# Two down projections by seven block products in place of eight

## The chip, the cores and the metric

The kernel runs on one core of one Trainium2 chip. The metric is the device time of the whole program in microseconds (us): the median of the runs.

## The reference

A trunk of two decoder layers on 512 tokens with 1024 features, in float32. Each layer mixes tokens in three branches (RWKV-7, retention, spatial gating), merges them by gates, and then runs a gated MLP with a causal convolution. The change is in the last product of that MLP:

```python
def conv_ffn(h, w_up, conv_w, conv_b, w_down):
    S = h.shape[1]
    u = h @ w_up
    up = jnp.pad(u, ((0, 0), (CONV_WIDTH - 1, 0), (0, 0)))
    c = conv_b
    for j in range(CONV_WIDTH):
        c = c + conv_w[j] * up[:, j:j + S]
    gate, val = jnp.split(c, 2, axis=-1)
    return (jax.nn.silu(gate) * val) @ w_down

# per layer, after the mixer:
x = x + conv_ffn(rmsnorm(x, norm2_g[l]), ffn_w_up[l], ffn_conv_w[l], ffn_conv_b[l], ffn_w_down[l])
# after both layers:
return rmsnorm(x, final_g)
```

`w_down` has 2816 rows (22 blocks of 128) and 1024 columns, so a down projection is (512 x 2816) by (2816 x 1024).

## The kernel before

The stream between layers is kept by features: eight tiles `x[m]` of 128 features by 512 tokens. A float32 product is made of three matmuls in the rounded type fp32r (`mm3`): each operand is split into a high part (a copy on ACT that rounds) and a low part (a subtraction on DVE), and the products high by low, high by high and low by high are added in PSUM. `unit` fetches a weight block of 128x512 by a DMA on SP's queue (`load`), splits it (`part`), and runs ahead of its use by a plan that a first pass over the program has noted; how far ahead depends on the pool (`AHEAD`). The order in which each engine gets its instructions is set by the Tile scheduler, except where `keep_in_program_order` fixes it.

Buffers of 128x512 float32: `u` has 31, `r` 16, `f` 39 (the MLP's), the split weights `wh` and `wl` three each. PSUM has four banks named `acc` and four named `sm`.

`ffn_up` makes 22 tiles of activations (128 features by 512 tokens). For each of the two columns of a tile it evacuates PSUM (L1054, DVE), applies the convolution (L1056 on ACT, L1057 and L1058 on DVE), then the gate (L1062 to L1064), and splits the result into `ah` tiles (L1066 ACT, L1067 DVE).

`ffn_down` (layer 0) has the weights as stationary operand and the activations as moving operand: for each of the eight output tiles, 22 blocks by three matmuls of 512 token columns, 528 in all. Behind each tile DVE adds it to x (L1078), and the norm of the next layer is prepared (`norm_z`, `norm_sq`).

`last` (layer 1) turns it around, so that the output has tokens in the partitions: a block of 128 tokens of the activations is stationary, and 512 output features of the weights are moving; 2 halves by 22 blocks by 4 token blocks by 3, 528 matmuls. The last `KEPT` blocks of the second half are done token block by token block, so that the final norm and the output of one overlap with the products of the next.

## Time and profile before

| | |
|---|---|
| Median of three runs | 1715.23 us (1712.87 to 1715.34) |
| Profiled execution, first to last instruction | 1712.1 us |
| Granted TensorE clock, mean | 1.000 |
| Layer 0 down projection on TensorE | 738.8 to 858.6 us |
| Layer 1 down projection on TensorE | 1585.8 to 1705.6 us |
| Behind the last matmul | 6.5 us |

For the profiled execution the page gives its span and no other time. PE is TensorE's matmuls, PEld its weight loads, DVE VectorE, ACT ScalarE, POOL GpSimd, SP the engine that issues most DMAs. A row for a group of instructions gives the line of the kernel, the engine, the operation, output and inputs by the program's names, the shape and the count, then busy time and the mean duration of one in ns; where a row answers a question on one line, it has the shortest, median and longest duration. A row of the timeline begins with the start in us and the duration in us; "x4" at its end says that four instructions are merged.

### The profile page before, as it was taken

Reading aid. Unit: us, or ns where it says so; the run is one execution under the profiler, and the core shown is the slowest. Engines: PE = TensorE matmul, PEld = TensorE weight load, DVE = VectorE, ACT = ScalarE, POOL = GpSimd, SP = SyncE. Lnnn points to the kernel's source line nnn. Section 1 sums busy time; section 2 is a strip of 40 time slices with the busy share of each in tenths; the row PEclk is TensorE's granted clock in tenths of the full one; section 3 lists DMA queues with packets and bytes.
Section 4 is the critical chain, followed back from the end, with each engine's and each line's share of the span. In section 5 each row is a group of like instructions: output and inputs, shape, how many; then the busy total and the mean of one; then the engine's idle time right before and its main releaser. Section 6 shows DMA issues by size and latency. Waiting matters only on the chain.

```text
span 1712.1 us, 27377 instructions
## 1 busy us (share of the span) xinstructions
PE 1701.0 (99%) x10280; PEld 1392.4 (81%) x10280; DVE 1155.0 (67%) x1998; ACT 774.9 (45%) x1315; POOL 178.2 (10%) x213
## 2 busy tenths in 40 slices
PE   9999999999999999999999999999999999999998
PEld 7888777788888888888888888777888888888886
DVE  6887745578669777753368887555776787787333
ACT  6563443554255444433355634345533554444223
POOL 2121000003200000000021210100141011100010
PEclk9999999999999999999999999999999999999999
DMA  5236553525542333233432365535254433333333
GB/s 180 87 109 205 174 174 99 178 89 163 163 148 93 98 99 96 69 113 114 123 105 87 107 222 168 159 122 178 77 185 147 137 122 117 113 109 99 99 99 105
DMA packets 132325, 219.61 MB, mean 128 GB/s; under 512 B 16864, under 2 KB 37088, under 8 KB 132192
## 3 DMA queue, kind: packets, MB, share of 16 engines
q1 hardware_dynamic: 116336, 180.94, 34.4%
q0 software_dynamic: 6784, 20.98, 3.8%
q10 hardware_dynamic: 9072, 15.94, 2.6%
q8 instruction: 81, 1.33, 0.3%
q14 instruction: 52, 0.43, 0.1%
HBM read 188.43 MB, written 29.36 MB: 127 GB/s over the span
## 4 chain that ended last, share of the span: by engine, by line
PE 89%; DMA 5%; DVE 3%; ACT 1%; issue 1%; SPq 1%; ACTq 0%; POOL 0%; DVEq 0%; POOLq 0%
PE acc L152 80%; PE sm L152 4%; PE sm L640 2%; DMA wr<-wall 2%; PE sm L893 1%; DVE wl L136 1%; PE sm L547 1%; DMA ws<-sgw 1%; DMA tr<-yt 0%; DMA tr<-bkT 0%; SPq L226 0%; DMA bkS<-tr 0%; PE sm L998 0%; DMA x<-xT 0%; DMA tr<-qkt 0%
## 5 line engine op out<-in xcount | busy, mean ns | idle before, releaser
L152 PE MATMUL acc<-hi,sh 128*128 128x512 f32 x1108 | 431.9, 390 | 0.0
L152 PE MATMUL acc<-lo,sh 128*128 128x512 f32 x1108 | 431.6, 390 | 0.0
L152 PE MATMUL acc<-hi,sl 128*128 128x512 f32 x1108 | 430.6, 390 | 0.0
L135 ACT CAST sh<-wr 128x512 fp32r<-128x512 f32 (+1 forms) x347 | 212.2, 615 | 356.6 <-PE acc L152 264.3
L136 DVE TENSOR_TENSOR sl<-wr,sh 128x512 fp32r<-128x512 f32 (+1 forms) x347 | 236.1, 683 | 139.9 <-ACT sh L135 74.9
L136 DVE TENSOR_TENSOR wl<-wr,wh 128x512 fp32r<-128x512 f32 x233 | 165.2, 710 | 184.9 <-ACT wh L135 182.3
L135 ACT CAST wh<-wr 128x512 fp32r<-128x512 f32 x233 | 144.1, 619 | 281.1 <-PE acc L152 182.3
L152 PEld LDWEIGHTS acc<-hi,sl 128*128 128x128 f32 x1108 | 208.0, 188 | 43.7 <-DVE gth L1013 0.3
L152 PEld LDWEIGHTS acc<-lo,sh 128*128 128x128 f32 x1108 | 208.0, 188 | 43.6 <-issue 0.9
L152 PEld LDWEIGHTS acc<-hi,sh 128*128 128x128 f32 x1108 | 208.0, 188 | 43.6 <-issue 0.3
L152 PE MATMUL acc<-lo,wh 128*128 128x512 f32 x588 | 232.5, 395 | 0.5 <-DVE lo L211 0.3
L152 PE MATMUL acc<-hi,wl 128*128 128x512 f32 x588 | 230.3, 392 | 0.5 <-DVE wl L136 0.5
L152 PE MATMUL acc<-hi,wh 128*128 128x512 f32 x588 | 229.5, 390 | 0.0
L152 PEld LDWEIGHTS acc<-lo,wh 128*128 128x128 f32 x588 | 110.5, 188 | 26.3 <-DVE lo L211 1.6
L152 PEld LDWEIGHTS acc<-hi,wl 128*128 128x128 f32 x588 | 110.5, 188 | 25.9 <-DVE wl L136 2.3
L152 PEld LDWEIGHTS acc<-hi,wh 128*128 128x128 f32 x588 | 110.6, 188 | 22.4 <-issue 0.2
L152 PE MATMUL acc<-ah,sh 128*128 128x512 f32 x352 | 108.4, 389 | 0.0
L1054 DVE TENSOR_TENSOR fu<-acc,rsF 128x512 f32<-128x512 f32 x88 | 60.6, 688 | 56.4 <-PE acc L152 56.3
L1056 ACT ACTIVATE cv<-fu,pc 128x512 f32<-128x512 f32 x88 | 71.6, 816 | 46.7 <-DVE fu L1054 44.4
L1057 DVE SCALAR_TENSOR_TENSOR cv<-fu,pc,cv 128x511 f32<-128x511 f32 x88 | 65.8, 748 | 21.1 <-ACT cv L1056 20.6
L152 PE MATMUL acc<-wl,hi 128*128 128x512 f32 x192 | 78.3, 408 | 0.0
L152 PEld LDWEIGHTS acc<-ah,sh 128*128 128x128 f32 x352 | 66.1, 188 | 13.7
(312 smaller groups left out, 2345.4 us busy)
## 6 DMA issues: line engine op xcount, KB each, us to landing
wr<-wall SPq DMA_DIRECT2D x488, 256.0 KB, 2.7
gd<-gth ACTq DMA_DIRECT2D x48, 256.0 KB, 3.0
gth<-gd POOLq DMA_DIRECT2D x48, 256.0 KB, 3.6
wr<-wdt SPq DMA_DIRECT2D x44, 256.0 KB, 2.6
wr<-wdn SPq DMA_DIRECT2D x40, 256.0 KB, 2.7
tr<-bkT SPq DMA_DIRECT2D x16, 256.0 KB, 2.8
bkS<-tr SPq DMA_DIRECT2D x128, 32.0 KB, 2.5
tr<-vT SPq DMA_DIRECT2D x8, 256.0 KB, 2.6
```

What stands on the lines that cost most here:

```text
L135: self.kept(self.nc.scalar.copy(hi[:, :n], raw[:, :n]))
L136: self.kept(self.nc.vector.tensor_tensor(lo[:, :n], raw[:, :n], hi[:, :n], op=SUB))
L152: i = self.nc.tensor.matmul(*x, **y)
L547: i = T.matmul(pK[hv[1 - h], j, :], bk[hv[h], c, 1, :], x[hv[h], c, :], start=True, stop=True)
L640: po(T.matmul(o, l, r, start=start, stop=True, skip_group_check=True))
L893: po(T.matmul(X[h][:, i, :], lhsT, rhs, start=new[h], stop=stop, skip_group_check=True))
L1054: V.tensor_tensor(u, ps, self.rsF, op=MUL)
L1056: A.activation(t, u, AF.Identity, scale=self.p("cw2", j), bias=self.p("cb", j))
L1057: V.scalar_tensor_tensor(t[:, 1:], u[:, :511], self.p("cw1", j), t[:, 1:], op0=MUL, op1=ADD)
```

## The change

Both down projections are computed by the seven-product scheme of Strassen and Winograd on 2x2 blocks: the 512 tokens are halved (256 each), the 22 row blocks of the weights are taken as eleven pairs `q` (even and odd block), and the output features are halved. Each weight block of a pair is called b11, b12, b21, b22; four of the seven products (numbers 7, 5, 6, 4 in the code) take sums of weight blocks and sums of activation halves, three (1, 2, 3) take plain blocks or one sum.

- In `ffn_up`, `halves` makes the sums of activation halves for each pair on POOL, splits two of the resulting tiles into `act`, and writes the plain first halves (`ab`) and one more sum (`s4`) to DRAM by DMAs on POOL's queue. They are read back later and split (`back`, `back4`, and their like in `last`).
- `sums` loads four raw weight blocks, forms three sums on POOL and one on DVE, in place, and `ring` splits each.
- Layer 0: four blocks `m` of output features (a pair of x tiles each), each in three groups of 4, 4 and 3 pairs `q`. A first phase of 12 steps makes products 7, 5, 6, 4 and adds them into x; a second phase makes products 1, 3, 2 from plain weights, loaded again. The weights are stationary, and a matmul has 256 token columns. The output tiles come in the order 1, 0, 3, 2, and so on.
- Layer 1: the activations are stationary as before, with 512 features in a product. A first phase over the eleven `q` makes products 7, 5, 6, 4 for two token blocks each in all eight PSUM banks; then product 1, then 3 and 2. Token blocks 2 and 3 are finished after product 1; blocks 0 and 1 at the end, with `KEPT` of 5 in place of 6.
- A `stage` number keeps `unit` from loading the next layer's weights before the end of layer 0's down projection.

The weights of layer 0 are laid out for this in DRAM. The diff without the end of `last`, which keeps the old links for the norm and the output, and some helpers:

```diff
-KEPT = 6
+KEPT = 5
...
+            if u[6] > self.stage or self.npart > at and (self.npart - at > AHEAD[u[5]] or u[5] == "f" and self.fp is None):
                 break
-            while self.nraw < min(self.npart + NRAW, len(self.plan)):
+            while self.nraw < min(self.npart + NRAW, len(self.plan)) and self.plan[self.nraw][6] <= self.stage:
...
-            hi, lo = at(), at()
-            A.copy(hi, th)
-            V.tensor_tensor(lo, th, hi, op=SUB)
-            act.append((hi, lo))
+            if i % 2 == 0:
+                even = th
+            else:
+                act.append(self.halves(even, th, i // 2, at))
         return act
 
+    def halves(self, a, b, q, at):
+
+        P, h = self.nc.gpsimd, [slice(0, 256), slice(256, 512)]
+        s, d = [self.wp.tile([128, 512], F32, name=self.nm(t), tag=t, bufs=3) for t in ("wh", "wl")]
+        P.tensor_tensor(s[:, h[0]], a[:, h[1]], b[:, h[1]], op=ADD)
+        P.tensor_tensor(s[:, h[1]], s[:, h[0]], a[:, h[0]], op=SUB)
+        P.tensor_tensor(d[:, h[0]], b[:, h[0]], s[:, h[1]], op=SUB)
+        ab = self.dp.tile([128, 512], F32, name=self.nm("ab"))
+        if q % 2 == 0:
+            self.s4 = self.dp.tile([128, 512], F32, name=self.nm("s4"))
+        for o, i in ((ab[:, h[0]], a[:, h[0]]), (ab[:, h[1]], b[:, h[0]]), (self.s4[:, h[q % 2]], d[:, h[0]])):
+            P.dma_start(o, i)
+        P.tensor_tensor(b[:, h[0]], a[:, h[0]], a[:, h[1]], op=SUB)
+        return self.split(s, at), self.split(b, at), ab, self.s4
 
     def ffn_down(self, l, act, x, st):
-        nc, V = self.nc, self.nc.vector
+        nc, V, A, P, po = self.nc, self.nc.vector, self.nc.scalar, self.nc.gpsimd, self.tc.keep_in_program_order
         self.load_pc(l + 1)
-        xd = []
-        for m in range(8):
-            ps = self.acc()
-            self.matF(ps, ("wdn", l, m, 0), act)
-            V.scalar_tensor_tensor(x[m], ps, 0.5, x[m], op0=MUL, op1=ADD)
-            self.norm_z(st, x[m], "n1")
+        Q, G, h = NFF // 2, [range(0, 4), range(4, 8), range(8, 11)], [slice(0, 256), slice(256, 512)]
+        self.pin = True
+        nring = [0]
+
+        def ring(w, n):
+            nring[0] += 1
+            if nring[0] % 2:
+                hi, lo = [self.wp.tile([128, 512], F32R, name=self.nm(t), tag=t, bufs=3) for t in ("wh", "wl")]
+            else:
+                hi, lo = [self.u(dt=F32R, n=t) for t in ("sh", "sl")]
+            A.copy(hi[:, :n], w[:, :n])
+            V.tensor_tensor(lo[:, :n], w[:, :n], hi[:, :n], op=SUB)
+            return hi, lo
+
+        def raw(m, j, i, g, al):
+            w, n = al(n="raw"), 128 * len(G[g])
+            po(nc.sync.dma_start(w[:, :n], self.a["wdn"][l, m, j, i][:, 512 * g:512 * g + n]))
+            return w
+
+        def sums(m, g):
+
+            n = 128 * len(G[g])
+            b12, b22, b11, b21 = [raw(m, j, i, g, self.r) for j, i in ((0, 1), (1, 1), (0, 0), (1, 0))]
+            c = lambda t: t[:, :n]
+            P.tensor_tensor(c(b22), c(b22), c(b12), op=SUB)
+            P.tensor_tensor(c(b12), c(b12), c(b11), op=SUB)
+            V.tensor_tensor(c(b11), c(b11), c(b22), op=ADD)
+            P.tensor_tensor(c(b21), c(b21), c(b11), op=SUB)
+            return [ring(w, n) for w in (b22, b12, b11, b21)]
+
+        def prod(ps, w, xs, new):
+            for i, (q, (x, at)) in enumerate(xs):
+                ws, cs = slice(128 * i, 128 * i + 128), slice(at, at + 256)
+                self.mm3(ps, (w[0][:, ws], w[1][:, ws]), (x[0][:, cs], x[1][:, cs]), new and i == 0, q == Q - 1, skip_group_check=True)
+
+        ab, s4 = {}, {}
+
+        def back(q, al):
+            o = self.u(n="ab")
+            nc.sync.dma_start(o, act[q][2])
+            ab[q] = self.split(o, al)
+
+        def back4(q, n):
+            o, hi, lo = self.u(n="s4"), self.f(dt=F32R, n="hi"), self.f(dt=F32R, n="lo")
+            nc.sync.dma_start(o[:, :n], act[q][3][:, :n])
+            A.copy(hi[:, :n], o[:, :n])
+            P.tensor_tensor(lo[:, :n], o[:, :n], hi[:, :n], op=SUB)
+            s4[q] = s4[q + 1] = hi, lo
+
+        steps = [(m, g) for m in range(4) for g in range(3)]
+        W = [sums(*steps[0])]
+        for n, (m, g) in enumerate(steps):
+            if n + 1 < len(steps):
+                W.append(sums(*steps[n + 1]))
+            if g == 0:
+                pa, pb = self.acc(), self.acc()
+                out = {7: pa[:, h[0]], 6: pa[:, h[1]], 5: pb[:, h[0]], 4: pb[:, h[1]]}
+            w = dict(zip((7, 5, 6, 4), W.pop(0)))
+            for p in (7, 5, 6, 4):
+                i, at = {7: (1, 0), 5: (0, 0), 6: (0, 256), 4: (1, 256)}[p]
+                prod(out[p], w[p], [(q, (act[q][i], at)) for q in G[g]], g == 0 and p in (7, 5))
+            if m == 2:
+                back(g, self.r)
+            elif m == 3:
+                for q in ((3, 4, 5), (6, 7), (8, 9, 10))[g]:
+                    back(q, self.r if q == 3 else self.f)
+            if g < 2:
+                continue
+            v, x0, x1 = self.f(n="v") if m == 3 else self.u(n="v"), x[2 * m], x[2 * m + 1]
+            two = lambda t: t.rearrange("p (a t) -> p a t", a=2)
+            twice = lambda t: t.unsqueeze(1).to_broadcast([128, 2, 256])
+            A.activation(v[:, h[0]], out[6], AF.Copy, scale=0.5)
+            V.scalar_tensor_tensor(v[:, h[1]], out[7], 0.5, v[:, h[0]], op0=MUL, op1=ADD)
+            V.scalar_tensor_tensor(two(x1), twice(out[5]), 0.5, two(x1), op0=MUL, op1=ADD)
+            V.scalar_tensor_tensor(x0[:, h[1]], out[4], 0.5, x0[:, h[1]], op0=MUL, op1=ADD)
+            P.tensor_tensor(x1, x1, v, op=ADD)
+            P.tensor_tensor(x0[:, h[1]], x0[:, h[1]], v[:, h[1]], op=ADD)
+        for q in range(0, Q, 2):
+            back4(q, min(512, 256 * (Q - q)))
+        order = [(m, p, g) for m in range(4) for p in (1, 3, 2) for g in range(3)]
+        todo, units = iter(order), []
+
+        def more(n):
+            for _, (m, p, g) in zip(range(n), todo):
+                j, i = {1: (0, 0), 2: (1, 0), 3: (1, 1)}[p]
+                units.append(ring(raw(m, j, i, g, self.f), 128 * len(G[g])))
+
+        def finish(m):
+            self.norm_z(st, x[m], "n1", m)
             self.norm_sq(st, x[m])
             d = self.dp.tile([128, 512], F32, name=self.nm("xd"))
             nc.gpsimd.dma_start(d, x[m])
-            xd.append(d)
+            xd[m] = d
+
+        xd, st["z"] = [None] * 8, [None] * 8
+        more(2)
+        for m, p, g in order:
+            more(1)
+            x0, x1 = x[2 * m], x[2 * m + 1]
+            if p != 2 and g == 0:
+                ps = self.sm((128, 256))
+                one = ps if p == 1 else one
+            o = one if p == 2 else ps
+            prod(o, units.pop(0), [(q, {1: (ab[q], 0), 2: (ab[q], 256), 3: (s4[q], q % 2 * 256)}[p]) for q in G[g]], g == 0 and p != 2)
+            if g < 2:
+                continue
+            if p == 1:
+                V.scalar_tensor_tensor(two(x1), twice(o), 0.5, two(x1), op0=MUL, op1=ADD)
+                V.scalar_tensor_tensor(x0[:, h[1]], o, 0.5, x0[:, h[1]], op0=MUL, op1=ADD)
+            elif p == 3:
+                V.scalar_tensor_tensor(x1[:, h[0]], o, 0.5, x1[:, h[0]], op0=MUL, op1=ADD)
+                finish(2 * m + 1)
+                if m == 3:
+                    self.stage += 1
+                    if self.plan:
+                        pool, self.pool = self.pool, None
+                        self.ahead(len(self.used))
+                        self.pool = pool
+            else:
+                V.scalar_tensor_tensor(x0[:, h[0]], o, 0.5, x0[:, h[0]], op0=MUL, op1=ADD)
+                finish(2 * m)
+        self.pin = False
...
+        def sums(q):
+
+            b12, b22, b11, b21 = [raw(2 * q + j, n) for j, n in ((0, 1), (1, 1), (0, 0), (1, 0))]
+            P.tensor_tensor(b22, b22, b12, op=SUB)
+            P.tensor_tensor(b12, b12, b11, op=SUB)
+            V.tensor_tensor(b11, b11, b22, op=ADD)
+            P.tensor_tensor(b21, b21, b11, op=SUB)
+            return [ring(w) for w in (b22, b12, b11, b21)]
...
+        pss = {p: [(self.acc if p in (7, 5) else self.sm)() for _ in range(2)] for p in (7, 5, 6, 4)}
+        W, ab = [sums(0)], []
...
+        for q in range(Q):
+            if q + 1 < Q:
+                W.append(sums(q + 1))
+            s, t = act[q][:2]
+            w = dict(zip((7, 5, 6, 4), W.pop(0)))
+            for p in (7, 5, 6, 4) if q < Q - 1 else (6, 7, 5, 4):
+                x, at = {7: (t, 0), 5: (s, 0), 6: (s, 256), 4: (t, 256)}[p]
+                for r in range(2):
+                    prod(pss[p][r], x, at, r, w[p], q == 0, q == Q - 1)
+            o = self.u(n="ab")
+            nc.sync.dma_start(o, act[q][2])
+            ab.append(self.split(o, self.f))
...
+        seq = [(1, q) for q in range(Q)]
+        k0 = Q - KEPT
+        for g in range(0, k0, 3):
+            seq += [(p, q) for p in (3, 2) for q in range(g, min(g + 3, k0))]
+        kept = [(p, q) for p in (2, 3) for q in range(k0, Q)]
...
+        ahead(3)
+        v1, v2, v3 = [], [], []
+        for r in range(2):
+            e, f, g = [self.f(n=t) for t in ("v1", "v2", "v3")]
+            A.activation(e, pss[6][r], AF.Copy, scale=0.5)
+            plus(f, pss[7][r], e)
+            plus(g, pss[5][r], e)
+            plus(e, pss[4][r], f)
+            plus(f, pss[5][r], f)
+            addx(e, 0, 2 + r)
+            addx(f, 1, 2 + r)
+            addx(g, 1, r)
+            v1.append(e), v2.append(f), v3.append(g)
+        one = [self.sm() for _ in range(2)]
+        out = {1: one, 2: one, 3: [self.acc() for _ in range(2)]}
+        for p, q in seq:
+            ahead(1)
+            for r in range(2):
+                go(p, q, r, units[p, q])
+            if (p, q) != (1, Q - 1):
+                continue
+            for r in range(2):
+                plus(v3[r], one[r], v3[r])
+                plus(v1[r], one[r], v1[r])
+                plus(v2[r], one[r], v2[r])
...
```

More of the change, by code (lines that the diff above doesn't have):

```diff
@@ new lines, in last, with ring, raw @@
+        ss = self.small((128, NC), "fss", 1)
+        self.pin = True
+        nring = [0]
+        def ring(w):
+            nring[0] += 1
+            if nring[0] % 2:
+                hi, lo = [self.wp.tile([128, 512], F32R, name=self.nm(t), tag=t, bufs=3) for t in ("wh", "wl")]
+            else:
+                hi, lo = [self.u(dt=F32R, n=t) for t in ("sh", "sl")]
+            A.copy(hi, w)
+            V.tensor_tensor(lo, w, hi, op=SUB)
+            return hi, lo
+        def raw(k, h):
+            w = self.u(n="raw")
+            po(nc.sync.dma_start(w, self.a["wdt"][0, k][:, H[h]]))
+            return w
@@ new lines, in last, with ahead @@
+        kept = [(p, q) for p in (2, 3) for q in range(k0, Q)]
+        units, todo = {}, iter(seq + kept)
+        def ahead(n):
+            for _, (p, q) in zip(range(n), todo):
+                w = raw(2 * q + (p > 1), p == 3)
+                if (p, q) in kept:
+                    hi, lo = [self.u(dt=F32R, n=t) for t in ("sh", "sl")]
+                    A.copy(hi, w)
+                    V.tensor_tensor(lo, w, hi, op=SUB)
+                    units[p, q] = hi, lo
+                else:
+                    units[p, q] = ring(w)
@@ new lines, in go, with addx, plus @@
+        def go(p, q, r, w):
+            x, at = {1: (ab[q], 0), 2: (ab[q], 256), 3: (s4[q // 2], q % 2 * 256)}[p]
+            prod(out[p][r], x, at, r, w, q == 0 and p != 2, q == Q - 1, skip_group_check=p < 3)
+        def addx(y, h, c):
+            for j in range(4):
+                b = y[:, 128 * j:128 * j + 128].rearrange("p (a d) -> p a d", d=32)
+                P.tensor_tensor(b, b, self.xt[4 * h + j][:, c], op=ADD)
+        def plus(y, ps, z, rows=slice(0, 512)):
+            return V.scalar_tensor_tensor(y[:, rows], ps[:, rows], 0.5, z[:, rows], op0=MUL, op1=ADD)
```

151 lines of the change are left out of this document (78 added, 73 removed).

## The prediction

> **What bounds the kernel now.** I read the page first (engine totals, then the chain that ended last), then the table of busy time by stretch for the stages that the change touches, then single instructions.
>
> ```profile
> PE 1701.0 (99%) x10280; PEld 1392.4 (81%) x10280; DVE 1155.0 (67%) x1998; ACT 774.9 (45%) x1315; POOL 178.2 (10%) x213
> PE 89%; DMA 5%; DVE 3%; ACT 1%; issue 1%; SPq 1%; ACTq 0%; POOL 0%; DVEq 0%; POOLq 0%
> ```
>
> TensorE is busy for 99% of the span and carries 89% of the chain. Fewer or shorter matmuls shorten the kernel as long as nothing else becomes late. The next rows are the two down projections, first by the instructions that read the activations (`ah`), then with all engines; the third stretch of the second fence is the first 119.8 us before the second layer's down projection, still up projection.
>
> ```profile
> 738.80:858.70 119.90, 119.80 (x528) 98.87 (x527) 0.69 (x1) 0.62 (x1) 1.00 0.40 118
> 1585.80:1705.60 119.80, 119.80 (x528) 98.91 (x527) 0.69 (x1) 0.62 (x1) 1.00 0.30 97
> ```
>
> ```profile
> 738.80:858.70 119.90, 119.90 (x531) 99.28 (x530) 48.20 (x81) 38.20 (x65) 3.78 (x7) 1.00 0.40 118
> 1585.80:1705.60 119.80, 119.80 (x529) 98.91 (x527) 43.14 (x82) 36.49 (x65) 5.95 (x4) 1.00 0.30 97
> 1466.00:1585.80 119.80, 119.80 (x530) 99.01 (x528) 93.99 (x145) 55.19 (x87) 7.64 (x14) 1.00 0.36 109
> 1705.60:1712.10 6.50, 0.04 (x1) 0.00 (x0) 2.09 (x8) 2.22 (x7) 0.00 (x0) 0.90 0.42 151
> ```
>
> Columns: stretch, length, PE, PEld, DVE, ACT, POOL, granted clock, DMA share, GB/s. Each down projection is 528 matmuls of 512 columns in 119.8 us, so 0.227 us each, at the full granted clock and without a gap. DVE is busy there for 40%, POOL for 3 to 5%. There is room beside TensorE, and the question is whether the change needs more than that room.
>
> **Removed: one product in eight.** Layer 1 goes from 528 to 7 x 11 x 2 x 3 = 462 matmuls of 512 columns: 462 x 0.227 = 104.9 us, 15.0 us less. Layer 0 goes to 7 x 11 x 4 x 3 = 924 matmuls of 256 columns. No 256-column product of this type is in the trace. The nearest rows:
>
> ```profile
> 372.82 1.87 PEld L998 LDWEIGHTS sm<-ws,sgv 128*128 128x128 f32 x15
> 373.05 1.72 PE L998 MATMUL sm<-ws,sgv 128*128 128x128 f32 x14
> L998 PEld LDWEIGHTS sm<-ws,sgv x64: 187/192/192, 372.8 to 1241.7; 128*128 128x128 f32 x64
> L998 PE MATMUL sm<-ws,sgv x64: 270/275/275, 373.0 to 1241.8; 128*128 128x128 f32 x64
> ```
>
> Here weight blocks of 128x128 follow each other every (1.72 - 0.27) / 13 = 0.111 us although one load lasts 0.19, so loads overlap and a new block each 0.111 us is possible. Half of the 512-column time is 0.1135 us. Ends: 0.111 below, 0.188 above (no overlap of loads at all); I take 0.1135, because the row with overlapping loads is the nearest. Layer 0: 924 x 0.1135 = 104.9, again 15.0 us less. "TensorE: Matmul & The Clock Gate" of the Trainium skill (section Back-to-back issue gap) gives N / 2.4 + 2.5 ns, 216 ns for 512 and 109 for 256 columns. The trace has 227 for 512, so the page is 5% low here; by it layer 0 would take 100.9 and the sum would be 4 us lower. Both layers together: -30.0 us, if TensorE stays fed.
>
> **Added: sums and splits.** For each group of blocks the code now builds three weight sums on POOL and one on DVE, then splits four results (ACT copy, DVE subtract). Before, a block had only a copy and a subtract. The costs:
>
> ```profile
> L1016 POOL TENSOR_TENSOR gth<-gth,gth x16: 1277/1292/1670, 408.6 to 1302.2; 128x512 f32<-128x512 f32 x16
> L136 DVE TENSOR_TENSOR sl<-wr,sh x347: 417/685/1155, 46.7 to 1689.1; 128x512 fp32r<-128x512 f32 x166, 128x256 fp32r<-128x256 f32 x8
> 723.47 1.89 DVE L136 TENSOR_TENSOR sl<-wr,sh 128x512 fp32r<-128x512 f32 x3
> 1646.13 5.95 POOL L1123 TENSOR_TENSOR ya<-ya,fg 128x512 f32<-128x512 f32 x4 [132.26 <-ACT sq L1109]
> 1645.80 1.07 DVE L1106 SCALAR_TENSOR_TENSOR ya<-acc,xt 128x128 f32<-128x128 f32 x5
> 1646.79 1.18 DVE L136 TENSOR_TENSOR wl<-wr,wh 128x512 fp32r<-128x512 f32 x1
> 1649.26 1.66 DVE L136 TENSOR_TENSOR wl<-wr,wh 128x512 fp32r<-128x512 f32 x1 [0.50 <-ACT wh L135]
> ```
>
> The first three rows are the prices: a POOL sum of 512 columns 1.29 us, DVE subtracts in a row 1.89 / 3 = 0.63 us. The last four rows are what I lean on. From 1646.13 POOL runs four sums. The very subtract that the change multiplies, 0.68 us when alone, takes 1.18 and 1.66 us there, and ends half a microsecond after the POOL sum that was running. POOL's four take 5.95 us instead of 4 x 1.29 = 5.16, so each of the two subtracts that got in cost POOL 0.40. DVE work with one operand in PSUM (L1106) isn't stretched. So a POOL sum and a DVE instruction with both operands in SBUF exclude each other, and their times add up as on one engine: call it the pair.
>
> "SBUF — State Buffer" of the Trainium skill (section SBUF: two separate sides) says the same more strictly: the shared port is locked for the whole instruction and the loser fully blocks. Where the trace shows 0.40 for a subtract let in, that rule would charge 0.68, and the full step below would take 7.3 us instead of 6.3, some 20 us more over both layers.
>
> Layer 0, first phase (products 7, 5, 6, 4; 12 steps; raw weights in the `r` buffers). A full step has three POOL sums and five DVE instructions of the pair: 3 x 1.29 + 3 x 0.40 + 2 x 0.63 = 6.33 us. TensorE needs 48 x 0.1135 = 5.45. A step of three blocks costs some 0.8 of it (the 256-column subtract is 0.42 against 0.68), 5.1 against 4.1. At the end of each feature block POOL adds v to x1 and half of x0: about 2.1. Four blocks: 4 x (2 x 6.33 + 5.1 + 2.1) = 79.4, and 11 splits of the `ab` read back, 11 x 0.63 = 6.9: 86 us of the pair. The first step (6.3) is prepared under the up projection, and perhaps half of the second (3). Against that, the last pair of acts falls into the phase: four POOL instructions of 256 columns and some six DVE instructions, about 7. The last product follows its ring (1.0). 86 - 9 + 7 + 1 = 85 us, where TensorE alone needs 528 x 0.1135 = 59.9: **+25**. Ends: all DVE hidden but 0.40 each (71 x 0.40 + 51 = 79, so +19); the strict rule of full durations, +37.
>
> Layer 0, second phase: 36 splits and the norm work, POOL nearly free; TensorE needs 45.0 us, DVE some 36 x 0.63 + 16 x 0.7 = 34, so TensorE binds. But the six `s4` splits have their subtract on POOL: 6 x (1.29 + 0.40) = 10, queued on POOL behind the last adds (2). Product 3 wants them from 33 x 0.1135 = 3.7 us on, over another 3.4: **+5** (0 if they are placed earlier under other work, 8 if the adds are late).
>
> Layer 1, first phase: 11 x 6.33 + 11 x 0.63 - 9 + 7 + 1.4 = 76, TensorE 264 x 0.227 = 59.9. The `ab` splits are not needed before the second phase; with half of them going there, **+12** (5 to 20). Second phase: 33 splits, 6 of `s4`, 24 small POOL adds in 45 us: +1.
>
> Up projection: the two splits for two acts stay; `halves` adds four POOL instructions of 256 columns (some 3 us) and three POOL DMAs per 21.8 us. DVE is at 93.99 of 119.8, so 17.1 per 21.8, and comes to 20. Four accumulators hide that; with the change of stage, where the next layer's weights may load only 3.7 us ahead, +1. These are the rows for DMA and ACT:
>
> ```profile
> L135 ACT CAST sh<-wr 128x512 fp32r<-128x512 f32 (+1 forms) x347 | 212.2, 615 | 356.6 <-PE acc L152 264.3
> L1010 POOL DMA_DIRECT2D gth<-gd x48 | 26.6, 557 | 0.0
> wr<-wdn SPq DMA_DIRECT2D x40, 256.0 KB, 2.7
> GB/s 180 87 109 205 174 174 99 178 89 163 163 148 93 98 99 96 69 113 114 123 105 87 107 222 168 159 122 178 77 185 147 137 122 117 113 109 99 99 99 105
> ```
>
> ACT has 4 x 0.615 = 2.5 us per step, hidden. SP issues four loads of 256 KB per step, 1 MB in 6.3 us or 166 GB/s, and a slice of 43 us has shown 222; hidden, unless the buffers are short (a rival below). Writes of `ab` and `s4` on POOL: 3 x 0.56 per pair of acts, also hidden. The end after the last matmul (6.5 us) keeps its links: one 512-column evacuation replaces four of 128. Nothing.
>
> **Sum**: -30 + 25 + 5 + 12 + 1 + 1 = **+14 us**. Against the profiled execution's span that is 1712.1 + 14 = 1726; the span lies 3.1 us under the median of the runs (1715.23), so I give 1729 for the median. About 3.4 us (0.2%) is what a measurement of this kernel can tell from no change.
>
> **Rivals.**
> (A) The forecast, the pair binds: +4 to +26. For: the stretched rows above, and 86 us of pair work in 60. Against: only a handful of collisions are in the trace, each short.
> (B) The pair binds, but more of it lies under the up projection (the third stretch leaves 26 us of DVE free per 119.8) or under PSUM reads: -10 to +4. It decides if two to three steps per layer are ready at the start, 2 x 6.3 more in each layer: 14 - 25 = -11 at most.
> (C) Faster: collisions cost little because the two alternate and each engine's own queue is far enough ahead. DVE alone has 5 x 0.63 = 3.2 and POOL 3.9 per step of 5.45, both below TensorE. Then only the ends stay, -30 + 5 + 5 = -20, some 1695 (-30 to -10). It decides if a full step of the pair falls below 5.45, that is if a subtract beside a sum costs under 0.3 on average. The 1.66 us speak against it.
> (D) Buffers: in layer 0's last feature block `r` holds five act tiles and eight of `ab`, so 3 of 16 are left for four raws. Loading the fourth then waits for two POOL sums, a split and 2.7 us of landing: some 12 us a step instead of 6.3. For two steps that adds 10, with a late last act 10 more: 1739 to 1760. Against: this overlaps the wait for the pair.
> (E) 256 columns don't hide the weight load: 924 x 0.188 = 174, 69 us more, under which the pair's 25 disappear: 1729 + 69 - 25, about 1773. The 0.111 us speak against it.
> That fewer matmuls are executed follows from the loops and is not in doubt.
>
> **Numbers.** A 0.56, B 0.13, C 0.15, D 0.12, E 0.04. Slower by over 0.2%: A, D, E and a sliver of B, 0.73. Within: half of B, 0.06. Faster: C and the rest of B, 0.21. The range leaves out E, the top of D and the lower half of C: 1698 to 1750. The likeliest case alone: 1719 to 1741.
>
> **What would show it.** Right: in the first phase of each layer PE shows gaps of about 1 to 2 us per step whose releaser is DVE (the split's subtract) or POOL; mean DVE time of the split rises from 0.69 to about 1; POOL sums of 1.3 to 1.75; the first phases last some 85 and 72 us; matmuls of 256 columns start every 0.114 us. The second phases are dense. Wrong: first phases near 60 us, or releasers that are DMA (D), or dense matmuls of 256 columns at 0.15 us or more (E).

## The result, and the profile after

| | before | after |
|---|---|---|
| Median of the runs on the same chip | 1715.28 us (4 runs) | 1801.57 us (4 runs) |
| Ratio, with its 95% interval | | 1.0496 (1.0475 to 1.0518) |
| Profiled execution, first to last instruction | 1712.1 us | 1800.0 us |
| Granted TensorE clock, mean | 1.000 | 0.979 |

The forecast was 1729 us within 1698 to 1750. The direction holds, the size doesn't: 86 us instead of 14. First the page after, engine totals and the granted clock in 40 slices (PEclk, in tenths of full speed, where 9 stands for 0.90 and more):

```profile
PE 1717.5 (95%) x10610; PEld 1404.8 (78%) x10610; DVE 1342.2 (75%) x2133; ACT 831.8 (46%) x1424; POOL 426.3 (24%) x478
PEclk9999999999999999898999999999999999998998
```

PE falls from 99% to 95% of a longer span, and its busy time rises by 16 us although by the prediction there are 30 us less to multiply. The clock row dips in four slices of 45 us: the 17th and 19th, around layer 0's down projection, and the 37th and 40th, in layer 1's. The table of busy time by stretch, for the work ahead of each down projection, before and then after (columns as in the prediction):

```profile
0.00:738.70 738.70, 734.81 (x4622) 599.10 (x4623) 529.57 (x918) 353.50 (x598) 73.30 (x81) 1.00 0.42 130
858.60:1585.70 727.10, 726.33 (x4603) 595.00 (x4602) 532.05 (x910) 344.49 (x580) 95.19 (x121) 1.00 0.43 133
```
```profile
0.00:745.80 745.80, 740.11 (x4622) 599.90 (x4622) 547.08 (x915) 351.67 (x594) 123.47 (x152) 1.00 0.43 136
905.50:1642.90 737.40, 733.73 (x4603) 596.95 (x4602) 545.80 (x906) 341.76 (x576) 145.95 (x193) 1.00 0.44 137
```

The same matmuls take 7.1 and 10.3 us longer. The rest is in the down projections, here cut at the gaps of TensorE. The first four rows are layer 0 (159.7 us instead of 119.9), the next six layer 1 (150.2 instead of 119.8), the last is the tail (6.9 instead of 6.5):

```profile
745.80:756.80 11.00, 0.18 (x2) 0.04 (x1) 5.18 (x7) 3.19 (x5) 5.86 (x8) 0.75 0.11 35
756.80:843.20 86.40, 71.11 (x528) 67.59 (x528) 74.59 (x80) 30.94 (x58) 58.12 (x41) 0.93 0.50 146
843.20:850.10 6.90, 0.05 (x2) 0.05 (x1) 5.50 (x9) 6.36 (x13) 2.74 (x3) 0.52 1.05 386
850.10:905.50 55.40, 51.86 (x396) 50.49 (x397) 43.72 (x67) 29.11 (x52) 12.21 (x13) 0.93 0.56 184
1642.90:1654.10 11.20, 0.16 (x2) 0.04 (x1) 7.50 (x9) 4.25 (x7) 6.53 (x8) 0.62 0.71 250
1654.10:1721.50 67.40, 62.85 (x240) 45.03 (x240) 64.72 (x58) 28.72 (x49) 47.71 (x30) 0.96 0.62 196
1721.50:1725.10 3.60, 0.12 (x1) 0.00 (x0) 3.41 (x5) 1.36 (x4) 1.59 (x1) 0.86 0.70 203
1725.10:1754.20 29.10, 28.48 (x108) 21.95 (x108) 22.16 (x33) 15.51 (x31) 11.56 (x16) 0.90 0.49 159
1754.20:1764.20 10.00, 0.12 (x2) 0.05 (x1) 5.85 (x12) 4.61 (x11) 7.94 (x15) 0.70 0.26 93
1764.20:1793.10 28.90, 28.76 (x114) 22.77 (x114) 14.88 (x32) 12.14 (x25) 2.66 (x3) 0.93 0.28 92
1793.10:1800.00 6.90, 0.00 (x0) 0.00 (x0) 1.79 (x5) 2.22 (x7) 0.00 (x0) 0.69 0.21 76
```

The first phases (rows 2 and 6) last 86.4 and 67.4 us, near the 85 and 72 foreseen. What wasn't foreseen are the five stretches with almost no matmul, 42.7 us together, and a clock below 1.00 in every stretch behind one. Four short stretches of dense matmuls show how the clock comes back, two at the start of layer 0's second phase and two at the start of layer 1's first:

```profile
852.00:857.00 5.00, 5.00 (x25) 5.00 (x25) 5.00 (x4) 2.10 (x4) 5.00 (x4) 0.50 1.04 374
857.50:862.50 5.00, 5.00 (x44) 5.00 (x43) 4.95 (x9) 1.15 (x3) 1.00 (x1) 1.00 0.71 224
1654.50:1659.00 4.50, 4.50 (x12) 3.44 (x12) 4.50 (x4) 1.86 (x3) 3.08 (x3) 0.50 0.28 87
1659.50:1664.00 4.50, 4.50 (x21) 3.60 (x20) 4.22 (x5) 1.77 (x3) 3.25 (x2) 1.00 0.58 169
```

For some 4 to 8 us behind a gap TensorE is dense at a granted clock of 0.50: 25 matmuls of 256 columns in 5 us, then 44. By the clock column, (1 - clock) times length over the five stretches of dense work, this lost 6.0 + 3.9 + 2.7 + 2.9 + 2.0 = 17.5 us; that is an upper estimate, because these stretches also hold short stops in which there was nothing to multiply. What the largest gaps wait for, from the waits of the weight loads, four answers for four windows (total, times, longest, us):

```profile
PEld acc L156 <- ACT wh L1104: 11.2, 1, 11.2
PEld sm L156 <- ACT wh L1104: 7.0, 1, 7.0
PEld acc L156 <- DVE wl L1235: 11.5, 1, 11.5
PEld sm L156 <- DVE wl L1235: 10.3, 1, 10.3
```

L1104 and L1235 are the splits of the weights (`ring`). Each row names the last link only. What stands in front of the first one is in POOL's timeline (start, duration, instruction, and in brackets the idle time before it and what ended it):

```profile
740.81 0.56 POOL L1087 DMA_DIRECT2D ab<-fth  x1 [11.58 <-DVE fth L1069]
750.44 0.71 POOL L1080 TENSOR_TENSOR wh<-fth,fth 128x256 f32<-128x256 f32 x1 [9.07 <-DVE fth L1069]
...
754.11 0.74 POOL L1088 TENSOR_TENSOR fth<-fth 128x256 f32<-128x256 f32 x1
754.79 1.27 POOL L1118 TENSOR_TENSOR raw<-raw,raw 128x512 f32<-128x512 f32 x1
756.14 1.61 POOL L1119 TENSOR_TENSOR raw<-raw,raw 128x512 f32<-128x512 f32 x1
```

L1080 to L1088 are `halves` for the last pair of activations, L1118 and L1119 the first step's sums. POOL waits 9.07 us for the last tile of activations (`fth`) and takes its instructions in order, so the sums start at 754.79, although the four raw blocks had landed by 742.4. TensorE's first matmul follows at 756.8.

In layer 1 the scheduler put the first of the sums (L1246) ahead of the last halves, and the gap is as long all the same:

```profile
1638.85 1.30 POOL L1246 TENSOR_TENSOR raw<-raw,raw 128x512 f32<-128x512 f32 x1
1648.69 1.27 POOL L1247 TENSOR_TENSOR raw<-raw,raw 128x512 f32<-128x512 f32 x1
1650.00 1.20 DVE L1248 TENSOR_TENSOR raw<-raw,raw 128x512 f32<-128x512 f32 x1 [2.63 <-POOL raw L1247]
1652.26 1.75 DVE L1235 TENSOR_TENSOR wl<-raw,wh 128x512 fp32r<-128x512 f32 x1
```

The second sum (L1247) waits on POOL behind the same halves. The split that the first product needs (L1235, of a block that was ready at 1640.2) stands on DVE behind the sum L1248, which waits for L1247. So two queues make this gap, POOL's and DVE's.

### The profile page after: what moved, and what is told of

Same layout as the page of the kernel before. It is cut to its first block, busy times and chain, and to the rows that moved or that the text cites. A ratio compares the mean times of both kernels' runs of the same rounds, so it can differ in the third digit from the quotient of the medians.

```text
span 1800.0 us, 28978 instructions
## 1 busy us (share of the span) xinstructions
PE 1717.5 (95%) x10610; PEld 1404.8 (78%) x10610; DVE 1342.2 (75%) x2133; ACT 831.8 (46%) x1424; POOL 426.3 (24%) x478
## 5 line engine op out<-in xcount | busy, mean ns | idle before, releaser
L139 ACT CAST sh<-wr 128x512 fp32r<-128x512 f32 x293 | 180.2, 620 | 287.4 <-PE acc L156 200.9
L140 DVE TENSOR_TENSOR sl<-wr,sh 128x512 fp32r<-128x512 f32 x293 | 212.0, 727 | 84.8 <-ACT sh L139 71.4
L140 DVE TENSOR_TENSOR wl<-wr,wh 128x512 fp32r<-128x512 f32 x195 | 137.2, 704 | 129.2 <-ACT wh L139 126.5
L139 ACT CAST wh<-wr 128x512 fp32r<-128x512 f32 x195 | 120.1, 619 | 217.8 <-PE acc L156 135.8
L1061 ACT ACTIVATE cv<-fu,pc 128x512 f32<-128x512 f32 x88 | 71.6, 816 | 96.5 <-DVE fu L1059 95.7
L1062 DVE SCALAR_TENSOR_TENSOR cv<-fu,pc,cv 128x511 f32<-128x511 f32 x88 | 75.1, 854 | 24.6 <-ACT cv L1061 24.3
L1063 DVE SCALAR_TENSOR_TENSOR cv<-fu,pc,cv 128x510 f32<-128x510 f32 x88 | 77.5, 880 | 1.2
L156 PE MATMUL acc<-wh,lo 128*128 128x512 f32 x196 | 76.6, 391 | 0.0
```

The source lines that it names most:

```text
L139: self.kept(self.nc.scalar.copy(hi[:, :n], raw[:, :n]))
L140: self.kept(self.nc.vector.tensor_tensor(lo[:, :n], raw[:, :n], hi[:, :n], op=SUB))
L156: i = self.nc.tensor.matmul(*x, **y, **kw)
L1061: A.activation(t, u, AF.Identity, scale=self.p("cw2", j), bias=self.p("cb", j))
L1062: V.scalar_tensor_tensor(t[:, 1:], u[:, :511], self.p("cw1", j), t[:, 1:], op0=MUL, op1=ADD)
L1063: V.scalar_tensor_tensor(t[:, 2:], u[:, :510], self.p("cw0", j), t[:, 2:], op0=MUL, op1=ADD)
```

## The experiments

The theory after this reading has five parts: (1) the first sums stand on POOL behind the last halves; (2) POOL and DVE exclude each other; (3) queues and buffers at the changes of phase; (4) `halves` on POOL hold up the up projection; (5) part of the 7 to 10 us ahead of the down projections comes from an address, because a removed small tile moves the `f` buffers, in the program's layout of a partition, from byte 146752 to 146720, 32 bytes off a multiple of 64. The rival to each is that another wait of the same length stands right behind. Where two medians are given, they are from runs on the same chip. A gain on after compares two chips; by the ratios it comes out within 1.3 us of the difference of the medians. A gap is counted below from the end of one matmul to the start of the next; so counted, the two start gaps of after are 10.8 and 11.0 us.

**e1, the first step early** (`ffn_down` and `last` as generators that stop behind the first sums):

```diff
+            if i == NFF - 1:
+                next(down)
```

> The loads, sums and splits of the first step of each layer are issued ahead of the last pair of activations instead of behind it; nothing else changes. Theory Q (queue): the first sums are late because POOL takes its instructions in order and they stand behind the last pair's halves, which wait for the end of the up projection. Then the gap of TensorE at the start of the down projections falls from 11.0 and 11.2 us to under 3, the clock stays at 1.0 there, and the kernel takes 1776 to 1786 us. Theory B (backlog): the pair of DVE and POOL is full in any case, so the first phases (86.4 and 67.4 us) grow by what the gaps lose, and the kernel takes 1796 to 1803.

1794.60 against 1714.56, ratio 1.0463 (1.0441 to 1.0484). The start gaps are gone, and behind the first step there is a new one, from the waits of the weight loads in layer 0:

```profile
PEld acc L156 <- ACT wh L1103: 8.1, 1, 8.1
```

TensorE stands for 7.9 us there and for 8.1 in layer 1: now the second step's sums stand behind the same last halves (on POOL they start at 759.55, right behind them). The wait is in POOL's order and not in the loads; one step early moves it. The gain is some 6 us, at the edge of the noise (the interval overlaps that of after), and the time lies between the two expectations.

**e2, all sums on DVE:**

```diff
-            P.tensor_tensor(c(b22), c(b22), c(b12), op=SUB)
+            V.tensor_tensor(c(b22), c(b22), c(b12), op=SUB)
```

and so the other two of a step, in both layers.

> The three weight sums per step go from POOL to DVE; nothing else changes. Theory L (lock): POOL sums and DVE instructions with both operands in SBUF exclude each other, so a step costs 3 x 1.29 + 3 x 0.40 + 2 x 0.63 = 6.3 us; on DVE alone it costs 8 x 0.63 = 5.0, under TensorE's 5.45 to 5.7. Then the first phase of layer 0 falls from 86.4 to 66 to 70 us, that of layer 1 from 67.4 to 61 to 64, the steps of layer 1 from 6.9 to 5.5 to 5.8 us, and with shorter gaps at the starts the kernel takes 1755 to 1775. Rival (DVE itself is the bound, with full durations of 0.68 and the splits of what is read back): steps of 6.1 and more, 1785 to 1800.

1776.65 against 1714.56, 1.0354 (1.0336 to 1.0372). The first phases by stretch:

```profile
757.00:831.40 74.40, 68.96 (x528) 67.08 (x528) 65.87 (x110) 31.38 (x58) 7.68 (x6) 0.94 0.55 164
1641.70:1706.60 64.90, 64.19 (x264) 51.26 (x264) 63.35 (x102) 35.04 (x62) 0.00 (x0) 0.96 0.71 226
```

Layer 0's takes 74.4 instead of 86.4 with the same work. Layer 1's takes 64.9 for all 264 products, where after took 67.4 for 240, a gap of 3.6 and 24 more behind it. DVE does the work of both engines in less time than the two took side by side. That alone could also come from fewer hand-overs between them; that they exclude each other is in the durations of single instructions. The same split in layer 1's first phase, in after beside POOL's sums and in e2 without them:

```profile
1671.45 1.78 DVE L149 TENSOR_TENSOR lo<-ab,hi 128x512 fp32r<-128x512 f32 x1
1666.71 0.69 DVE L149 TENSOR_TENSOR lo<-ab,hi 128x512 fp32r<-128x512 f32 x1
```

The pair is real. DVE then is busy for 63.35 of 64.9, so nothing is left to gain on this way. The start gaps stay (12.8 and 10.6), as DVE too gets the sums behind the last activations. The time lies just above the 1755 to 1775 expected: layer 0's phase takes 74.4 and not 66 to 70.

**e3, the four instructions of `halves` on DVE:**

```diff
-        P.tensor_tensor(s[:, h[0]], a[:, h[1]], b[:, h[1]], op=ADD)
+        self.nc.vector.tensor_tensor(s[:, h[0]], a[:, h[1]], b[:, h[1]], op=ADD)
```

> The four sums and differences of activation halves per pair go from POOL to DVE; the weight sums stay on POOL. Theory Q: the stops of TensorE late in both up projections (2.4 and 2.3 us, with a half clock behind them) and part of the gaps at the starts of the down projections come from halves that wait for each other in POOL's queue and hold splits on ACT and DVE; they get shorter by 10 to 20 us in all: 1780 to 1790. Rival: DVE has 17 us of work in 21.8 there and four more instructions of 0.4 us each make it as late as POOL did: 1797 to 1805.

1791.19 against 1714.56, 1.0436 (1.0414 to 1.0457). In after, both up projections have a stop of 2 us near their end, with 3.4 us at half clock behind it. TensorE waits there for the split of a weight block on ACT (L139), and ACT's order shows why it is late; the first of the two:

```profile
729.26 0.62 ACT L148 CAST ah<-fth 128x512 fp32r<-128x512 f32 x1 [1.46 <-POOL fth L1088]
729.79 1.65 ACT L139 CAST sh<-wr 128x512 fp32r<-128x512 f32 x3
```

It stands behind a split of activations that waits for `halves` on POOL. In e3 the stops are gone, and the start gaps shrink to 9.5 and 7.9. That is 10 us in all, at the low end of what was expected.

**e4, layer 1 alone** (`ffn_down` and the split of activations as before for layer 0):

```diff
+        if l == 0:
+            ...
```

> Layer 0 keeps the eight products of before; only layer 1 has seven. By the stretches of the two traces layer 0's down projection costs 40.0 us more than before and layer 1's 30.2, its up projection 4 and the end 0.6; if the parts add up, this kernel takes 1748 to 1756. Rival: what layer 0 leaves behind (buffers and the order of the queues in layer 1) makes part of layer 1's loss; then under 1742.

1759.14 against 1714.56, 1.0255 (1.0239 to 1.0271), a little above what was expected. The gaps of layer 1 are those of after. The miss is in the part that was taken as unchanged: layer 0's old down projection takes 123.2 us instead of 119.9, with no gap. That pointed to part 5.

**e5, the `f` buffers back on a multiple of 64 bytes**, and **e6, the kernel before with its buffers 32 bytes off it:**

```diff
-            ss = self.small((128, NC), "fss", 1)
+            ss, pad = self.small((128, NC), "fss", 1), self.small((128, NC), "fbi", 1)
+            nc.vector.memset(pad, 0.0)
```
```diff
+        V.memset(self.small((128, 8), "pad", 1), 0.0)
```

> The change no longer has the small tile of four floats that held the bias of the final norm; the buffers f, which are allocated behind the small tiles, thereby start 32 bytes lower, at 146720 in place of 146752 bytes of a partition, no longer a multiple of 64. This kernel puts a tile of that size back (cleared once), nothing else. Theory A (address): the 1816 matmuls of 512 columns that start every 0.233 us instead of 0.227 in the changed kernel do so because an operand in f lies off the 64-byte grid; they return to 0.227, 1816 x 0.0067 = 12 us, of which 9 to 14 come off the time (256-column products may gain too): 1787 to 1793. Rival (the slower spacing comes from more traffic in SBUF, or from the granted clock): spacing stays at 0.233, 1799 to 1803.

> The kernel before, with one small tile of eight floats more (cleared once), so that f starts 32 bytes off the 64-byte grid; nothing else. Theory A: its matmuls with an operand in f (both down projections with 1056, and the merges, some 1850 in all) go from 0.227 to 0.233 us and the kernel from 1715 to 1725 to 1729. Rival: no change, 1713 to 1718.

e6: 1730.54 against 1717.02, 1.0076 (1.006 to 1.0092). The instructions that read `ah` in its two down projections:

```profile
744.90:868.10 123.20, 123.09 (x528) 98.84 (x528) 0.69 (x1) 0.62 (x1) 1.00 0.39 115
1600.20:1723.40 123.20, 123.10 (x528) 98.98 (x527) 0.69 (x1) 0.62 (x1) 1.00 0.31 94
```

528 matmuls take 123.2 us instead of 119.9: 0.2333 us each instead of 0.227, at full clock, without a gap, in a kernel that differs by one tile that is cleared and not used. e5: 1793.52 against 1717.02, 1.0448 (1.0425 to 1.0472), 8 us less than after, just under the 9 to 14 expected. In a stretch of the merges (330 to 440 us) 568 matmuls run, as in before (567; after has 562). In layer 1's first phase the spacing comes back in part only, to 0.230 on average, for which no run gives the reason; in e9 and e14 below it is 0.227 there too. Matmuls of 256 columns don't change.

**e7, three of the small sums of the second token block in `r` instead of `f`:**

```diff
-            e, f, g = [self.f(n=t) for t in ("v1", "v2", "v3")]
+            e, f, g = [(self.r if r else self.f)(n=t) for t in ("v1", "v2", "v3")]
```

> In layer 1 the three tiles v1, v2, v3 of the second token block come from the buffers r, of which eight are free, instead of f, where 22 tiles of ab, 12 of s4 and 6 of v ask for 39 places; nothing else. Theory F (places): the gap of 10.3 us ahead of the first product 2 is there because the second block's evacuations wait for a place in f, and DVE's later splits stand behind them. It goes, with 2 us of half clock behind it: 1787 to 1791. Rival (POOL's chain of small adds is what is late): the gap stays at 8 to 10 us, 1798 to 1803.

1797.39 against 1717.02, 1.0469 (1.0451 to 1.0487). In layer 1's second phase 22 + 12 + 6 = 40 tiles want the 39 buffers of `f`, and the long gap (9.9 us; 10.3 by the weight loads) was the wait for one. The waits of the weight loads from 1715 to 1760:

```profile
PEld sm L156 <- DVE wl L1235: 7.7, 3, 4.0
```

In its place are gaps of 3.1 and 2.4 us, so it gives 4 us and not the 11 to 15 expected. The interval overlaps that of after, and in the two profiled executions only 2.7 us of the gain lie in layer 1's down projection.

**e8, three weight blocks of layer 0's second phase split ahead of the `ab` and `s4` read back last:**

```diff
+            if (m, g) == (3, 2):
+                more(3)
             if m == 2:
                 back(g, self.r)
...
-        more(2)
```

> In layer 0 the loads and splits of the first three weight units of the second phase are issued ahead of the last read-backs of ab and s4; nothing else. Theory Q (queue): the 7.1 us between the phases is ACT working through five ab copies and six s4 copies, some of which wait for their loads, before the copy that TensorE waits for. The gap falls under 2 us and the time by 6 to 9, to 1792 to 1796, unless product 3 then waits for s4. Rival: it moves to the first product 3, 1799 to 1803.

1791.73 against 1717.02, 1.0433 (1.0417 to 1.0448). The lines that `more` needs move up with it. The gap at the change falls from 6.9 to 0.6 us, with one of 1.5 behind it, and that of 2.8 us near the end of the phase goes as well. The gain is 10 us in all, where 6 to 9 were expected; in the two profiled executions 5.7 of it lie in layer 0's down projection, and 2.4 ahead of it, where the edit changes nothing. The wait was not for POOL's `s4` subtracts but in ACT's and DVE's order: the splits of `ab` and `s4` stood ahead of the weights'.

**e9, e2 + e3 + e5 + e7 + e8 together.**

> Five of the edits together: weight sums on DVE, halves on DVE, f back on the 64-byte grid, v of the second token block in r, the second phase's first rings ahead of the read-backs. Alone they gave about -25, -10, -8, -4 and -10 us. If the losses are separate, 1745 plus or minus 5. Rival (they hide each other: with more on DVE the phases are held by DVE instead of the pair): 1755 to 1765.

1753.54 against 1716.2, 1.0216 (1.0198 to 1.0234). The five gains add up to 57 us, measured 48; the time lies between the two expectations. Start gaps of 11.2 and 8.9 remain.

**e10, e9 with the first step of layer 0 and two of layer 1 early** (and the raw blocks of layer 0's last feature block in `u` in place of `r`):

```diff
+            if i in ((NFF - 3, NFF - 1) if l else (NFF - 2, NFF - 1)):
+                next(down)
```

> The five edits, and the first step of layer 0 and the first two of layer 1 prepared under the up projection (issued ahead of the last one or two tiles of it), and the raw weights of layer 0's last feature block in u, where places are free. Theory Q: the gaps at the starts (9 to 11 us each) mostly go, since TensorE has work while the last pair of activations is made: 1722 to 1732. Rival (DVE is at its limit in the up projection, so what is done early delays the up projection by as much): 1738 to 1745.

1743.69 against 1716.2, 1.0165 (1.015 to 1.018): the rival holds. The stretches with the two new stops, and layer 1's first phase:

```profile
744.90:751.50 6.60, 0.28 (x3) 0.08 (x1) 4.88 (x15) 1.85 (x3) 1.08 (x2) 0.68 0.27 85
...
1590.00:1594.00 4.00, 0.53 (x4) 0.10 (x2) 3.85 (x8) 1.82 (x4) 1.08 (x2) 0.98 0.17 61
1609.00:1677.90 68.90, 64.39 (x265) 49.80 (x264) 63.15 (x103) 35.45 (x60) 1.08 (x2) 0.98 0.73 243
```

In layer 0 the gap stands behind the one early step, as in e1; in layer 1 two early steps take DVE's time from the up projection, which stops at 1590 for 3.5 us, and didn't stop there in e9.

**e11 to e13, layer 1 alone, repaired:** sums on DVE, `v` in `r`, `f` aligned, two steps early; `halves` on POOL (e11) or DVE (e12), or as e11 with the early steps spread over the tiles (e13):

```diff
-            if i in (NFF - 3, NFF - 1):
+            if i in (NFF - 5, NFF - 2):
```

> Seven products in layer 1 alone, layer 0 as before; f on the 64-byte grid, sums on DVE, v of the second block in r, two steps ahead, halves still on POOL. TensorE saves 15.0 us there. What is left by the theories: nearly full DVE in the first phase (9 x 0.63 = 5.7 per 5.45, +3), the stop late in the up projection (+4), a start of 2 to 4, changes of phase 3 to 5, the end 0.5. Sum -15 + 14 = about 0: 1709 to 1718. Rival (DVE's early work delays the up projection as well): 1720 to 1728.

> As the one before, with the halves on DVE too. If the stop late in the up projection comes from halves queued on POOL, it goes (-3 to -5): 1705 to 1714. Rival: DVE has 20 of 21.8 us there and the two early steps on top, so it is as late as before: 1712 to 1722.

> As e11, with the two early steps issued at tiles 17 and 20 of the up projection in place of 19 and 21. If the stop of 6.2 us late in the up projection is DVE's early work bunched together, it shrinks to under 3 and the clock stays up: 1721 to 1726. Rival (any early work costs the same, since DVE is at its limit): 1727 to 1732.

1728.82 (1.0076, 1.0059 to 1.0093) and 1726.46 (1.0065, 1.005 to 1.008) against 1716.2, and 1727.85 (1.0075, 1.0058 to 1.0092) against 1714.61. Among the three nothing can be told apart. The intervals lie above 1. None came down to where its theory put it (1709 to 1718, 1705 to 1714, 1721 to 1726); e13 fits its rival, and e11 and e12 lie above theirs too. The up projection stops for 5.8, 3.5 and 6.7 us, in e11 here:

```profile
PEld acc L156 <- ACT sh L139: 6.3, 1, 6.3
```

Wherever the early steps are put, the up projection pays for them.

**e14, e10 without any weight sums** (`pass` in place of the eight lines, so its output is not the product):

> As e10, with the weight sums left out in both layers (the raw blocks are split as they are), so that a step has four DVE instructions in place of eight; TensorE's products are the same in number and size. Theory D (DVE is what is left): first phases near TensorE's own time, 528 x 0.119 = 63 and 264 x 0.227 = 60 us, the starts without gaps: 1705 to 1718. Rival (loads, places and the order of the phases): first phases stay at 70 and more, 1730 to 1740.

1724.68 against 1714.61, 1.0056 (1.0041 to 1.0071). Its first phases, to a few us, by stretch:

```profile
739.00:805.00 66.00, 61.48 (x491) 60.98 (x490) 45.36 (x77) 32.11 (x61) 8.40 (x8) 0.95 0.62 200
1590.00:1655.00 65.00, 63.15 (x272) 51.79 (x271) 38.55 (x64) 30.56 (x54) 1.63 (x3) 0.97 0.80 263
```

In layer 1, DVE is busy for 39 us of 65 here, after 63 of 69 in e10, and the kernel gains 19 us on e10: that is what the weight sums still cost there. It stays 10 us above before with no sums at all, between the two expectations. From first to last matmul the first phases last 70.7 and 63.4 us, so layer 0's fits the rival and layer 1's the theory. Gaps of 3.2 us behind the early step and of 6.3 and 2.4 at layer 1's change remain, each with half clock behind it. They say what the 10 us are. The two down projections last 126.9 + 123.3 us, where 924 x 0.12 + 462 x 0.227 = 215.8 would be dense: of the 34.4 between them, gaps over 0.3 us are 20.5, and half clock outside them cost 11.9. No version was faster than before.

## Why the prediction was right and wrong

Right: slower, and the pair as a cause (e2). Its price fits as well: a step of layer 1's first phase lasts 6.92 us (from one sum L1246 at 1669.24 to the next at 1676.16), where the prediction's 6.33 and one split of 0.63 make 6.96. The lengths of the first phases agreed: 86.4 for 85, and 67.4 for 72 less the 24 products that moved behind it, 72 - 24 x 0.227 = 66.6. But the agreement in layer 0 is partly luck: e2 takes out 12.0 us with the pair, of the 25 assigned to it. The rest is half clock (e2's 0.06 x 74.4 = 4.5), matmuls that start later than taken (below), and DVE's own load, 65.87 of 74.4.

The forecast had +14, the spans differ by 87.9. By stretches the 74 between them are 22.2 us at the two starts, 2.2 in the first phases, 32.5 in the second phases, 16.4 in the work ahead and 0.4 at the end. By steps of the prediction:

- **"The first step (6.3) is prepared under the up projection": this failed, and cost the two longest gaps, 11.0 + 11.2 us.** The loads were early, as said, but in layer 0 all the sums are behind the last `halves` in POOL's order, and those wait for the last tile; in layer 1 all but the first are, and DVE's order holds the split of that one. The prediction listed what POOL executes and not in which order. e1 shows the place; e10 and e13 show that preparing more isn't free either, so rival B's condition (two or three steps ready at the start) has a price that it left out.
- **The changes of phase, priced at 5 and 1 us.** Layer 0: the gap is 6.9 us, near the price, but by another mechanism (e8). With that the second phase takes 6.9 + 55.4 = 62.3 instead of 50; of the 12.3 the gap is 1.9, the half clock 3.9, a gap of 3.1 at 900.6, behind a late weight load, is the next, the spacing of 256 columns 396 x 0.0065 = 2.6, and 0.8 stay unassigned. Layer 1: 3.6 + 29.1 + 10.0 + 28.9 = 71.6 instead of 45 + 1 + 5.4 = 51.4; of the 20.2 the gaps are 13.6 (e7 bears on the longer), the half clock 4.9, the spacing of 0.2333 by the address 222 x 0.0066 = 1.5.
  Rival D had the right kind of cause, too few buffers; in layer 1 it was in `f`, which D didn't name. In layer 0, `r` does run short in the last feature block, as D says. SP waits there up to 4.6 us for a place (until DVE's sum L1120 is done with one), and POOL's last sum then waits for its fourth block:

```profile
POOL raw L1121 <- DMA raw<-wdn: 3.5, 1, 3.5
```

But TensorE's gaps there are 1.5, 2.6 and 1.4 us, 5.5 together, and not the 10 to 20 of D.

- **The granted clock wasn't in the sum at all.** 17.5 us in the down projections, by the rows above. No stretch of before shows it in the middle of the work, because TensorE had no gap there; with the tail's 0.90 the prediction had the only sign of it in hand.
  "TensorE: Matmul & The Clock Gate" of the Trainium skill (section Part 1: The HAM clock gate) says that the array falls to half rate after an idle window of about 3.4 us and needs a busy one to return, with windows that run free. The trace agrees in part: 0.50 behind the gaps of 3.6 to 11.2 us, for 4 to 8 us of matmuls, then 1.00. At half rate these are 2 to 4 us on top of each gap. But a shorter gap can be enough: behind the stop of 2.0 us at 728.4 the clock is 0.50 as well.

```profile
730.80:734.20 3.40, 3.40 (x10) 2.53 (x9) 1.99 (x4) 0.64 (x2) 0.00 (x0) 0.50 0.45 146
```

It is so behind a gap of 2.6 us at 824.9, too, while in e8 the same stop of 2.0 us (at 727.4) has 1.00 behind it. So its length alone doesn't decide about a short gap, and a run's time differs by some us with it.

- **The up projection, priced at +1 over both layers:** stops of 2 us in each with half clock behind them, together 7 to 8 us (e3 removes the stops); most of the rest is the address, next. TensorE's four accumulators did not hide POOL's `halves`.
- **An address.** A tile that is no longer allocated put the `f` buffers off a multiple of 64 bytes: 8 us (e5), the reverse of which cost before 13.5 us (e6). It explains why work that the change doesn't touch became slower.
- **256 columns: 0.120 us and not 0.1135.** The products of layer 0's second phase in a dense stretch, with full clock:

```profile
864.90:889.90 25.00, 24.84 (x207) 24.37 (x205) 3.71 (x8) 0.00 (x0) 1.00 0.51 164
```

24.84 / 207 = 0.120, so 924 x 0.0065 = 6.0 us more, and layer 0 saves 9 us and not 15. Rival E (0.188) is out. The estimate of 109 ns that follows for 256 columns from the formula of the Trainium skill for a matmul by itself ("TensorE: Matmul & The Clock Gate", section Back-to-back issue gap) is 9% low here.

Not settled: what the steps cost one by one, as gaps and clock overlap, and the stretches alone add up; the price of the short `r`, as e10 moves those blocks together with other edits; and layer 1's spacing in e5.

## What to carry to other kernels

When TensorE is busy for 99% of the span, fewer products only pay if every other engine's queue, read in order, has the next operand ready at each change of stage: write down the order of the queue and what its first instruction waits for, not only the busy time. A gap of TensorE of 3.6 us and more cost its length here and then 2 to 4 us at half clock, so one long gap and its price should be looked for first. When work that an edit doesn't touch becomes slower by 3%, look at the addresses of its operands.

## What the runs showed of the hardware that was not expected

- Matmuls with 512 fp32r columns start every 0.2267 us with `f` buffers on a multiple of 64 bytes and every 0.2333 us 32 bytes off it (119.9 against 123.2 us for 528; in e6 the whole kernel takes 0.76% longer, 0.6 to 0.92). Those of 256 columns show 0.12 us in both. Other offsets were not tried.
- POOL sums of 128x512, 1.29 us alone, have a median of 1.74 us in layer 1's first phase, beside DVE's splits; the line of the first of them (shortest, median, longest in ns, then first and last start):

```profile
L1246 POOL TENSOR_TENSOR raw<-raw,raw x11: 1292/1742/1754, 1638.9 to 1717.6; 128x512 f32<-128x512 f32 x11
```

That is 0.45 us for each, near the 0.40 of the prediction: letting a DVE instruction end first costs POOL less than that instruction's 0.68. The whole 0.68, as the Trainium skill has it ("SBUF — State Buffer", section SBUF: two separate sides), doesn't show in this row. Nor does it in the step: three sums and six DVE instructions one after the other would make 3 x 1.29 + 6 x 0.63 = 7.65 us (0.63 for one of several in a row, as in the prediction), and it lasts 6.92.
